# A decayed running sum over a matrix product: seven block products in one of 32 groups, and a list scheduler for slots 34 to 243

## The chip, the cores and the metric

One Trainium2 core runs the whole kernel. The metric is the device time of one launch in microseconds (us), lower is better. Engines: PE (TensorE, matmuls into PSUM), DVE (VectorE), ACT (ScalarE), POOL (GpSimd) and SP, which here only issues the stores.

## What is computed

```python
B, S, D = 16, 2048, 1024          # x: B x S x D, w: D x D, decay: D, all float32
xw = x @ w
out[:, 0, :] = xw[:, 0, :]
for t in range(1, S):
    out[:, t, :] = decay[None, :] * out[:, t - 1, :] + xw[:, t, :]
```

So there is one large product (32768 x 1024 by 1024 x 1024) and, down each column of each batch, a linear recurrence in time. The constants lie between 0.05 and 0.95, one for each column.

## The kernel before

**Tiling.** Time is cut into 64 chunks of 512 steps, and two chunks of one batch make a group: 32 groups. In each group there are eight tiles, one for each n, the block of 128 output columns; a tile is 128 columns by 1024 time steps, since columns lie on partitions and time runs along them. `slots` numbers the tiles: slot s is group s // 8 and n = s % 8. (The last group is worked as two single chunks, slots 248 to 263.) Group 14 is slots 112 to 119; it is the first half of a batch.

**One chunk of x** passes through four steps. `load` (L105) is four POOL DMAs that also turn it into bf16 (xb, three buffers). `turn` (L115) is a transpose on DVE (xw, two buffers). `part` (L123) is two ACT copies that sort it into xt (bf16, 4 x 2 x 512 columns, five buffers). Then 128 matmuls read each pair of chunks. In the written orders these are the letters L, T, X and Y.

**One tile.** PE does 16 matmuls of 128 x 128 by 512 columns (L131), eight blocks k of the inner size for each of the two chunks, into one of three PSUM buffers ps of two banks. Then the recurrence follows in one of two ways:

- A *paired* tile (three of four) solves pairs of steps. ACT copies ps to xs (`copy`, L185, letter p; three buffers) and makes g, the even-numbered steps times decay (`odd`, L170, g). POOL adds g to the odd-numbered steps (`join`, L205, j). DVE scans those 512 values with the squared decay (`scan`, L210, S). ACT scales the result (`even`, L170, h) and POOL adds it to fill the other half (`fill`, L253, c). g and h take turns in four buffers h. A small ACT copy or POOL memset (`zero`, L201 or L199, z) sets the value before the tile.
- An *unpaired* tile (one of four, n % 4 = 3) is one DVE scan of 1024 steps straight from ps (L228).

Either way the last value is kept for the next group of the batch (`save`, L257, k; only in the first half of a batch). DVE transposes the finished line so (four buffers) into ot (`back`, L265, B). After four tiles, SP stores ot (four buffers) in four DMAs (L289). The squared decays lie in a PSUM bank, so that the short scan has one operand there.

**What sets the order.** Every instruction is pinned to the order in which the program issues it, on each engine by itself; buffers and data make engines wait for each other by semaphores. Around slots 0 to 33 and from slot 244 on, the order is written out by hand in `agenda`, a list of letters for each slot. In between `usual` (L522) writes it by one rule: the tile's own copy, scaled half and join, then scan, end and outgoing transpose of the tiles before, then the chunk work that `later` has put at that slot, then one or two loads. `rest` (L536) does what is left over at slot 244.

Of the kernel before, what the change touches and what calls it, by code (L numbers as in the profile page):

```python
# [25 lines left out]
def kernel(  # L26
# [41 lines left out]
    CR = CH // NQ  # L68

# [24 lines left out]
    def ot_tile(nj):  # L94
        return ring(sb, "ot", 4, [128, nj, CR])

# [22 lines left out]
    def part(c, copy, m0, m1, j0=0, j1=NJ):  # L119
        if c not in xt_of:  # L120
            xt_of[c] = ring(sb, "xt", 5, [128, M, 2, TL], BF16)
        src = xw_of[c][:, m0:m1, j0:j1].rearrange("p m j i e -> p m e (j i)")
        pin(copy(out=xt_of[c][:, m0:m1, :, j0 * P:j1 * P], in_=src))  # L123
# [17 lines left out]
    class Tile:  # L141
# [3 lines left out]
        def __init__(self, g, n, ps, outlets):  # L145
# [7 lines left out]
            self.lot = sum(t.paired for t in tiles)  # L153
            self.prev = None if self.t0 == 0 else last[n]
            if self.t0 + self.T < S:
                last[n] = const.tile([128, 1], FP32, name=f"keep{n}", bufs=2)
                self.keep = last[n]
            else:
                self.keep = None

        @property
        def so(self):
            if not hasattr(self, "held"):
                self.held = sb.tile([128, 2 * TL + 2], FP32, name=f"so{self.turn % 4}")
            return self.held

        def decayed(self, src, h=None):
            if h is None:
                h = ring(sb, "h", 4, [128, TL])[:, 0:self.T // 2]
# [12 lines left out]
        def copy(self):  # L182
            self.xs = sb.tile([128, 2 * TL], FP32, name=f"xs{self.lot % 3}")[:, 0:self.T]
            for t, ps in self.parts():
                pin(nc.scalar.copy(out=self.xs[:, t:t + ps.shape[1]], in_=ps))  # L185

        def odd(self):
            self.g = ring(sb, "h", 4, [128, TL])[:, 0:self.T // 2]
            for t, ps in self.parts():
                size = ps.shape[1]  # L190
                self.decayed(ps[:, 0:size:2], self.g[:, t // 2:(t + size) // 2])

# [3 lines left out]

        def zero(self):
            if self.prev is None:
# [4 lines left out]
        def join(self):  # L203
            odds = self.xs[:, 1:self.T:2]
            pin(nc.gpsimd.tensor_tensor(out=odds, in0=self.g, in1=odds, op=ALU.add))  # L205

        def scan(self):
            T, n, so = self.T, self.n, self.so
            if self.paired:
# [3 lines left out]
                    data1=self.xs[:, 1:T:2],  # L213
                    initial=0.0 if self.prev is None else self.prev,
# [7 lines left out]
        def run(self, ps, t, size):  # L222
# [3 lines left out]
            else:  # L226
                before = 0.0 if self.prev is None else self.prev
# [13 lines left out]
        def complete(self):  # L241
# [3 lines left out]
            if self.keep is not None:  # L245
                self.save()

        def even(self):
            self.h = self.decayed(self.so[:, 1:self.T + 1:2])

        def fill(self):
            T = self.T
            pin(nc.gpsimd.tensor_tensor(  # L253
                out=self.so[:, 2:T + 2:2], in0=self.h, in1=self.xs[:, 0:T:2], op=ALU.add))

        def save(self):
            pin(nc.scalar.copy(out=self.keep, in_=self.so[:, self.T + 1:self.T + 2]))  # L257
# [15 lines left out]
    class Outlet:  # L273


        def __init__(self, ns, nj, half=0, queues=(nc.sync,), pieces=1):
# [3 lines left out]
            self.ot = ot_tile(nj)  # L280
# [135 lines left out]
    def turn_and_load(c):  # L416
# [61 lines left out]
        21: "p20 g20 L S18 X8 j20 B17 B19",  # L478
        22: "L h18 p21 c18 B16 k18 g21 B18 Y8 z20 L j21 S20",
        23: "p22 z21 z22 S21 L h20 g22 T9 c20 h21",  # L480
        24: "k21 k20 j22 S23 X9 L c21 Y9 B20 L",
        25: "B23 k23 p24 B21 g24 z24 j24 S22 z25",
        26: "p25 T10 k22 h22 g25 c22 S24 X10 j25",
        27: "B22 p26 S25 g26 z26 Y10 j26",
# [4 lines left out]
        32: "c29 S31 S30 h30 B29 c30 p32 g32 z32 j32 B30 B31 L L",  # L489
        33: "p33 g33 z33 j33 S32 h32 c32 k32 L L",  # L490
# [22 lines left out]
    later = {}  # L513
    begun = {"T": 12, "X": 11, "Y": 11}
    for c in range(5, nch):
        first = c // 2 * K
        ahead = (7, 6, 4) if c % 2 else (11, 10, 8)
        for letter, a in zip("TXY", ahead):
            if c >= begun[letter]:
                later.setdefault(first - a, []).append(f"{letter}{c}")  # L520

    def usual(s):  # L522
        paired = [t.paired for t in tiles]
        do = [f"P{s}"] if paired[s] else []
        if paired[s - 1]:
            do.append(f"S{s - 1}")
        if not paired[s]:
            do.append(f"S{s}")
        do.append(f"C{s - 1}")
        if paired[s - 2]:  # L530
            do.append(f"B{s - 2}")
        if not paired[s - 1]:
            do.append(f"B{s - 1}")
        return do + later.get(s, []) + ["L"] * (2 if len(loads) > NQ else 1)

    def rest(s):  # L536
        do = [f"S{s - 1}"] if tiles[s - 1].paired else []
        do.append(f"C{s - 1}")
        if tiles[s - 2].paired:
            do.append(f"B{s - 2}")  # L540
        return do + [f"B{s - 1}"] + later.get(s, []) + ["L"] * len(loads)

# [3 lines left out]

    perform(agenda[-99].split())
    spares = [spare] + [ring(psp, "spare1", 1, [128, TL])]
    for step, (g, n) in enumerate(slots):
        T = TL * len(g)  # L550
        left = step - len(slots)
        if n % R == 0:
            ns, nj = range(n, n + R), T // P
            outlets = [Outlet(ns, nj)]
# [54 lines left out]
        do = agenda.get(step, agenda.get(left) if left >= -20 else None)  # L609
        if do is None:  # L610
            do = usual(step)
# [34 lines left out]
```

## Time and profile before

| | before |
|---|---|
| median of 3 runs | 904.96 us (904.68 to 905.02) |
| the profiled execution | 905.68 us |
| its span | 903.9 us |
| busy: PE, DVE, ACT, POOL | 896.4, 825.5, 686.3, 656.7 us |
| granted PE clock | 0.999 |
| matmuls | 4217 recorded |
| DMA | 204.77 MB moved, 227 GB/s in the mean |
| a load of x: issue to landing | 7.9 us in the median |
| a store: issue to landing | 10.9 us in the median |

The profile is one execution, recorded instruction by instruction. A line names a group: source line, engine, operation, what is written and read, shape, count, then busy time, mean time of one in ns and the idle time of the engine ahead of it, with the one that ended it. Starts of neighbours on one engine can lie closer than a duration, since the next instruction begins before the last one has quite ended. The span is the profile's own; the device time has some 1.8 us around it.

### The profile page before, as it was taken

The numbers are of one execution on the slowest core, as the hardware profiler recorded it, in microseconds if no ns is written. First come the engines' busy times: TensorE is split into PE (matmuls) and PEld (weight loads), VectorE is DVE, ScalarE is ACT, GpSimd is POOL, SyncE is SP. The second block draws the span as 40 slices with busy tenths as digits, with TensorE's granted clock in tenths as the row PEclk, the third lists the DMA queues.
The fourth block names the chain that finished last, engine by engine and source line by source line (L and its number), as shares of the span: only waits on it lengthen the run. The fifth ranks groups of instructions, "written<-read, shape, count | busy, mean of one in ns | idle before, by whom it ended". The sixth has DMA issues, their size and how long they took to land.

```text
span 903.9 us, 12113 instructions
## 1 busy us (share of the span) xinstructions
PE 896.4 (99%) x4217; PEld 412.7 (46%) x4217; DVE 825.5 (91%) x628; ACT 686.3 (76%) x957; POOL 656.7 (73%) x755
## 2 busy tenths in 40 slices
PE   8999999999999999999999999999999999999997
PEld 5544444444444444444444444444444444444444
DVE  4999998999999999999998999999999999999997
ACT  4899967777877877877778778778777787787742
POOL 7978678777767768677677677777777776776632
PEclk9999999999999999999999999999999999999999
DMA  9999999999999999999999999999999999999868
GB/s 186 190 215 215 226 256 217 215 237 236 254 242 260 243 251 257 248 237 226 224 237 229 224 229 229 230 224 229 231 227 228 233 232 222 226 233 211 176 143 235
DMA packets 402542, 204.77 MB, mean 227 GB/s; under 512 B 8752, under 2 KB 401456, under 8 KB 402480
## 3 DMA queue, kind: packets, MB, share of 16 engines
q1 hardware_dynamic: 265168, 134.76, 61.0%
q0 software_dynamic: 137024, 68.70, 56.6%
q8 instruction: 33, 0.54, 0.2%
q10 hardware_dynamic: 288, 0.52, 0.2%
q14 instruction: 29, 0.24, 0.1%
HBM read 138.42 MB, written 134.22 MB: 302 GB/s over the span
## 4 chain that ended last, share of the span: by engine, by line
PE 97%; DMA 1%; POOL 0%; issue 0%; DVE 0%; DVEq 0%; POOLq 0%
PE ps L131 96%; DMA xb<-in_x_dram 1%; PE spare L131 1%; POOL xb L105 0%; PE spare L395 0%; PE ps L395 0%; DVE h L399 0%; DVE xw L115 0%; DVEq L115 0%; POOLq L630 0%
## 5 line engine op out<-in xcount | busy, mean ns | idle before, releaser
L131 PE MATMUL ps<-xt,wsb 128*128 128x512 bf16 (+1 forms) x4028 | 866.3, 378 | 0.0
L131 PEld LDWEIGHTS <-wsb 128*128 128x128 bf16 x4168 | 407.5, 98 | 478.0 <-ACT wsb L313 0.8
L205 POOL TENSOR_TENSOR xs<-h,xs 128x512 f32<-128x512 f32 (+1 forms) x190 | 242.8, 1278 | 188.1 <-ACT h L170 85.3
L185 ACT COPY xs<-ps 128x1024 f32<-128x1024 f32 (+1 forms) x190 | 188.9, 994 | 152.9 <-PE ps L131 148.1
L265 DVE STREAM_TRANSPOSE ot<-so 128x1024 f32<-128x1024 f32 (+1 forms) x260 | 300.0, 1191 | 2.1 <-POOL so L199 1.1
L253 POOL TENSOR_TENSOR so<-h,xs 128x512 f32<-128x512 f32 (+1 forms) x190 | 241.0, 1270 | 43.7 <-ACT h L170 27.8
L123 ACT COPY xt<-xw 128x2048 bf16<-128x2048 bf16 (+3 forms) x136 | 242.3, 1790 | 8.7 <-DVE xw L115 8.7
L105 POOL DMA_DIRECT2D xb<-in_x_dram x264 | 174.0, 660 | 5.6 <-DMA xb<-in_x_dram 3.2
L170 ACT ACTIVATE h<-so,dec 128x512 f32<-128x512 f32 (+1 forms) x190 | 145.3, 766 | 28.7 <-DVE so L210 25.2
L115 DVE STREAM_TRANSPOSE xw<-xb 128x2048 f32<-128x2048 f32 (+3 forms) x78 | 147.4, 1901 | 8.0 <-DMA xb<-in_x_dram 7.9
L210 DVE TENSOR_TENSOR_SCAN so<-spare,keep,xs 128x512 f32<-128x512 f32 (+1 forms) x97 | 119.9, 1239 | 26.7 <-POOL xs L205 26.4
L210 DVE TENSOR_TENSOR_SCAN so<-spare,xs 128x512 f32<-128x512 f32 x93 | 113.3, 1219 | 27.4 <-POOL xs L205 24.5
L170 ACT ACTIVATE h<-ps,dec 128x512 f32<-128x512 f32 (+1 forms) x190 | 130.0, 684 | 0.0
L228 DVE TENSOR_TENSOR_SCAN so<-dec,ps 128x1024 f32<-128x1024 f32 x34 | 76.8, 2260 | 1.0 <-ACT h L170 1.0
L228 DVE TENSOR_TENSOR_SCAN so<-dec,keep,ps 128x1024 f32<-128x1024 f32 (+1 forms) x35 | 75.9, 2168 | 0.2 <-issue 0.2
L257 ACT COPY keep<-so 128x1 f32<-128x1 f32 x136 | 25.3, 188 | 9.5 <-DVE so L228 9.0
L201 ACT COPY so<-keep 128x1 f32<-128x1 f32 x97 | 18.4, 191 | 2.7 <-DVE ot L265 2.4
L131 PE MATMUL spare<-xt,wsb 128*128 128x512 bf16 (+3 forms) x60 | 12.6, 329 | 0.0
L131 PE MATMUL ps<-xw,wsb 128*128 128x256 bf16 (+3 forms) x68 | 11.2, 301 | 0.4 <-DVE xw L115 0.4
L199 POOL MEMSET so<- 128x1 f32 x93 | 10.7, 117 | 0.6 <-DVE ot L265 0.6
L331 PE MATMUL spare<-idle 128*128 128x512 bf16 x22 | 6.8, 479 | 1.2 <-DVE idle L321 1.2
L306 POOL DMA_DIRECT2D ot<-in_w_dram x12 | 6.6, 552 | 1.7 <-DMA xb<-in_x_dram 0.8
(39 smaller groups left out, 37.9 us busy)
## 6 DMA issues: line engine op xcount, KB each, us to landing
out_dram<-ot SPq DMA_DIRECT2D x248, 512.0 KB, 10.9
xb<-in_x_dram POOLq DMA_DIRECT2D x248, 256.0 KB, 7.9
out_dram<-ot SPq DMA_DIRECT2D x12, 256.0 KB, 4.2
ot<-in_w_dram POOLq DMA_DIRECT2D x12, 128.0 KB, 5.6
xb<-in_x_dram POOLq DMA_DIRECT2D x8, 128.0 KB, 5.4
out_dram<-xb SPq DMA_DIRECT2D x3, 256.0 KB
xb<-in_x_dram POOLq DMA_DIRECT2D x4, 144.0 KB, 7.0
ot<-in_w_dram ACTq DMA_DIRECT2D x2, 256.0 KB, 5.2
```

Of the source, the lines that this page charges most:

```text
L105: pin(nc.gpsimd.dma_start(out=xb_of[c][quad(q), j0:j1], in_=_ap(x, [[D, P], [P * D, j1 - j0], [1, CQ]], (b * S + t0 + j0 * P) * D + q * CQ)))
L115: pin(nc.vector.transpose(out=dst.rearrange("p (m j i) -> p j m i", m=M, i=P)[:, j0:j1, m0:m1], in_=src.rearrange("p (j m c) -> p j m c", ...
L123: pin(copy(out=xt_of[c][:, m0:m1, :, j0 * P:j1 * P], in_=src))
L131: pin(nc.tensor.matmul(out=ps[:, t0:t1] if ps.shape[1] >= t1 else ps, lhsT=lhs, rhs=rhs, start=(k == 0 and t0 == start), stop=(stop and k ...
L170: pin(nc.scalar.activation(out=h, in_=src, func=mybir.ActivationFunctionType.Copy, scale=dec[:, self.n:self.n + 1]))
L185: pin(nc.scalar.copy(out=self.xs[:, t:t + ps.shape[1]], in_=ps))
L205: pin(nc.gpsimd.tensor_tensor(out=odds, in0=self.g, in1=odds, op=ALU.add))
L210: pin(nc.vector.tensor_tensor_scan(out=so[:, 3:T + 2:2], data0=squares[-1][:, n:n + 1].to_broadcast([128, T // 2]), data1=self.xs[:, 1:T:2 ...
L228: pin(nc.vector.tensor_tensor_scan(out=so[:, t + 2:t + 2 + size], data0=dec[:, n:n + 1].to_broadcast([128, size]), data1=ps, initial=befor ...
L253: pin(nc.gpsimd.tensor_tensor(out=self.so[:, 2:T + 2:2], in0=self.h, in1=self.xs[:, 0:T:2], op=ALU.add))
L257: pin(nc.scalar.copy(out=self.keep, in_=self.so[:, self.T + 1:self.T + 2]))
L265: pin(nc.vector.transpose(out=outlet.ot[:, :, c0:c0 + P], in_=self.so[:, 2 + t0:2 + t0 + nj * P].rearrange("p (i t) -> p i t", t=P)))
```

## The change

**Seven products.** In group 14, tiles are worked in pairs (n = 0 and 1, 2 and 3, ...). Inner size, columns and the two chunks each split in two, so that a pair is a product of 2 x 2 blocks, and it is formed by seven block products instead of eight. A block product is four matmuls of 512 columns. It needs sums of x (three in a new buffer sx, one written over half of the group's second xt; each 128 x 2048 bf16; the first, second and fourth on DVE, the third on POOL, each after the one before) and differences of w (five for each pair, 20 in all, each 128 x 512 bf16, on POOL, spread over 80 us that begin 170 us before the group). The products a1, a2, a3 and a4 accumulate in one PSUM bank of a pair, b1 and b2 in the other, c in the bank spare0. Between them ACT copies partial results to the tile's line (A1, A2, B1, A4, "lift") and DVE adds or subtracts (C, A3, B2, "join"), and the next product of that bank waits for this. The tiles then go on as paired ones, without the copy p. All tiles of groups 13, 14 and 15 are paired.

**Order.** In slots 34 to 243 all work is made into jobs with an engine, a cost, a key (how urgent) and what must come before. `in_order` runs these through a list scheduler: an engine that is free takes the most urgent job that is ready. The order that results is issued; on the chip each engine keeps it and waits by semaphores as ever. At its start, ACT, DVE and POOL are taken as busy for 4.0, 4.5 and 5.5 us, and a sum of x on DVE is put at 2.15 us. One tile in five is unpaired where one in four was.

**Buffers.** xs goes; the copy p is written to so and the work is done there, in seven buffers (four so and three xs before). ot goes from four to three, xt from five to four. The transpose of a chunk is split in two halves. The hand-written slots 21 to 33 move X8 to Y9 later and leave X10, Y10 and the last loads to the scheduler.

```diff
+    OTS, XTS, SOS, HS = 3, 4, 7, 4
+    FROM, TO = 34, 244
+    SUMS, SUMT = ('dve', 'dve', 'pool', 'dve'), -24
+    WBY, WLEAD, WSTEP = "pool", 170, 4
+    SHARE = {-1: 0, 0: 0, 1: 0.06, 2: 0.2, 3: 0.2, 9: 0.2}
+    merged = (14,)
...
-        return ring(sb, "ot", 4, [128, nj, CR])
+        return ring(sb, "ot", OTS, [128, nj, CR])
...
-            xt_of[c] = ring(sb, "xt", 5, [128, M, 2, TL], BF16)
+            xt_of[c] = ring(sb, "xt", XTS, [128, M, 2, TL], BF16)
...
-        def copy(self):
-            self.xs = sb.tile([128, 2 * TL], FP32, name=f"xs{self.lot % 3}")[:, 0:self.T]
-            for t, ps in self.parts():
-                pin(nc.scalar.copy(out=self.xs[:, t:t + ps.shape[1]], in_=ps))
-
-        def odd(self):
-            self.g = ring(sb, "h", 4, [128, TL])[:, 0:self.T // 2]
-            for t, ps in self.parts():
-                size = ps.shape[1]
-                self.decayed(ps[:, 0:size:2], self.g[:, t // 2:(t + size) // 2])
-
...
+        def copy(self):
+            for t, ps in self.parts():
+                pin(nc.scalar.copy(out=self.line[:, t:t + ps.shape[1]], in_=ps))
+
+        def odd(self, spot=None):
+            src = self.line if isinstance(self.ps, tuple) or self.ps is None else self.ps
+            self.g = self.decayed(src[:, 0:self.T:2], spot)
...
-        21: "p20 g20 L S18 X8 j20 B17 B19",
-        22: "L h18 p21 c18 B16 k18 g21 B18 Y8 z20 L j21 S20",
+        21: "p20 g20 L S18 j20 B17 B19",
+        22: "L h18 p21 c18 B16 k18 g21 B18 z20 L j21 S20",
         23: "p22 z21 z22 S21 L h20 g22 T9 c20 h21",
-        24: "k21 k20 j22 S23 X9 L c21 Y9 B20 L",
-        25: "B23 k23 p24 B21 g24 z24 j24 S22 z25",
-        26: "p25 T10 k22 h22 g25 c22 S24 X10 j25",
-        27: "B22 p26 S25 g26 z26 Y10 j26",
+        24: "X8 k21 k20 j22 S23 Y8 L c21 B20 L",
+        25: "B23 k23 p24 B21 g24 z24 j24 S22 X9 z25",
+        26: "p25 T10 k22 h22 g25 c22 Y9 S24 j25",
+        27: "B22 p26 S25 g26 z26 j26",
...
+            for e, queue in ready.items():
+                if idle[e] > now:
+                    continue
+                kept = []
+                while queue and queue[0][2].takes and not spots:
+                    kept.append(heapq.heappop(queue))
+                job = heapq.heappop(queue)[2] if queue else None
+                for one in kept:
+                    heapq.heappush(queue, one)
+                if job is None:
+                    continue
+                if job.takes:
+                    job.spot = spots.pop(0)
+                order.append(job)
+                job.start = now
+                end = idle[e] = now + job.cost
+                if job.locks:
+                    idle["pool"] = max(idle["pool"], now) + job.cost / 2
+                heapq.heappush(events, (end, -1 - len(order), None))
+                for other in job.gives:
+                    heapq.heappush(events, (end + GAP, -1 - len(order), (other.spot,)))
...
+    GAP = 0.19
+    BEGUN = {"pe": 0.0, "act": 4.0, "dve": 4.5, "pool": 5.5}
+    LAND = 11.0
+    STORED = 13.0
+    PASS = 0.2158
+    cost = {"p": .91, "g": .6, "z": .12, "j": 1.27, "S": 1.16, "D": 2.2, "h": .68, "c": 1.27,
+            "k": .11, "B": 1.14, "T": 1.14, "X": 1.79, "L": .66, "half": .5, "both": .62,
+            "sum": 2.15, "wpool": 1.15, "wdve": 1.2, "slow": 4.2}
+    each = R * PASS
+
+    differences = ((1, 0, 1, 1), (1, 1, 0, 0), (0, 0, 0, 1), (0, 1, 1, 1), (1, 0, 0, 0))
+
+    def differ(d, j):
+        k1, n1, k2, n2 = differences[d]
+        one, two = (wsb[:, k * R:(k + 1) * R, n + 2 * j].rearrange("p k q i -> p k (q i)")
+                    for k, n in ((k1, n1), (k2, n2)))
+        by = nc.vector if WBY == "dve" else nc.gpsimd
+        pin(by.tensor_tensor(out=wd[:, d, j], in0=one, in1=two, op=ALU.subtract))
...
+        weights = []
+        for i in range(5 * R if merged else 0):
+            weights.append(Job(WBY, cost["w" + WBY], starts[min(merged)] - WLEAD + WSTEP * i,
+                               lambda i=i: differ(i % 5, i // 5)))
+            weights[-1].locks = WBY == "dve"
+            weights[-1].early = max(16.0, weights[-1].key - 4)
...
+        def chunk(c):
+            need = starts[c // 2] - 21 + (c % 2) * 8
+            if c > 11:
+                quads = [q for cc, q in loads if cc == c] if c <= 14 else range(NQ)
+                got = [Job("pool", cost["L"], need - 28 + 2.5 * q, lambda c=c, q=q: load(c, q),
+                           [turned.get(c - 3)]) for q in quads]
+                for q, a in zip(quads, got):
+                    a.early = max(4.0, need - 3 * 4 * each * R + 2) + q * each * R
+                ends = [(a, LAND + (3 if need < 60 else 0)) for a in got]
+                for half in range(2):
+                    turned[c] = Job(
+                        "dve", cost["T"], need + 2 * half,
+                        lambda c=c, h=half: turn(c, 0, NJ, h * M // 2, (h + 1) * M // 2),
+                        ends + [turned.get(c - 1), part_of.get((c - 2, 1)), turned.get(c)])
+                    if len(got) < NQ:
+                        turned[c].early = 2 * LAND
+                    part_of[c, half] = Job(
+                        "act", cost["X"], need + 3 + 3 * half,
+                        lambda c=c, h=half: part(c, nc.scalar.copy, h * M // 2, (h + 1) * M // 2),
+                        [turned[c], part_of.get((c - 1, half))] + used.get(c - XTS, []))
...
+        def solve(tile, ready, key, banks):
+            s = tile.turn
+            prev = place.get((tile.before.turn, "k")) if tile.before is not None else None
+            gone = place.get((s - SOS, "B"))
+            pos = lambda name, e, c, k, do, after, takes=False: place.setdefault(
+                (s, name), Job(e, cost[c], key + k, do, after, takes))
+            if not tile.paired:
+                end = pos("S", "dve", "D", 3, tile.scan, ready + [gone, prev])
+                banks.append(end)
+            else:
+                if tile.ps is not None or not tile.mixed:
+                    p = pos("p", "act", "p", 0, tile.copy, ready + [gone])
+                    banks.append(p)
+                    ready_xs = [p]
+                else:
+                    ready_xs = ready
+                g = pos("g", "act", "g", .5, None, ready, True)
+                g.do = lambda: tile.odd(g.spot)
+                banks.append(g)
+                z = pos("z", "pool" if tile.before is None else "act", "z", 1, tile.zero,
+                        ready_xs + [prev])
+                j = pos("j", "pool", "j", 1.2, tile.join, ready_xs + [g])
+                j.gives = (g,)
+                S = pos("S", "dve", "S", 1.5, tile.scan, [j, prev])
+                h = pos("h", "act", "h", 4.5, None, [S, z], True)
+                h.do = lambda: tile.even(h.spot)
+                end = pos("c", "pool", "c", 5.5, tile.fill, [h])
+                end.gives = (h,)
+            if tile.kept:
+                pos("k", "act", "k", 3.7, tile.save, [place[s, "S"]])
+            back(tile, end, key)
...
+            b = Job("dve", cost["B"], key + 8, tile.back,
+                    [end, place.get((s, "k"))] + stored.get(lump - OTS, []) + ([first] if first else []))
...
+        def product(out, xs, ws, begin):
+            for k in range(R):
+                pin(nc.tensor.matmul(out=out, lhsT=ws(k), rhs=xs[:, k // 2, k % 2],
+                                     start=begin and k == 0, stop=k == R - 1,
+                                     skip_group_check=True))
...
+            def sums(i, engine):
+                if i == 0:
+                    sx[0] = sb.tile([128, 3, 2, 2, TL], BF16, name="sx")
+                a, b = xt_of[c0], xt_of[c1]
+                S1, S2, S0 = (sx[0][:, k] for k in range(3))
+                out, one, two = ((S1, b[:, 0:2], b[:, 2:4]), (S2, a[:, 0:2], S1),
+                                 (S0, a[:, 2:4], S2), (b[:, 0:2], a[:, 0:2], b[:, 0:2]))[i]
+                flat = lambda x: x.rearrange("p m e t -> p (m e t)")
+                pin(engine.tensor_tensor(out=flat(out), in0=flat(one), in1=flat(two), op=ALU.add))
+
+            done = []
+            for i in range(4):
+                by = SUMS[i]
+                done.append(Job(by, cost["sum" if by == "dve" else "slow"], t + SUMT + i,
+                                lambda i=i: sums(i, nc.vector if SUMS[i] == "dve" else nc.gpsimd),
+                                parts + done[-1:] + used.get("sx", [])))
+                done[-1].locks = by == "dve"
...
+            what = {
+                "a1": ("a", lambda: S(0), w_at(0, n0), True, 0),
+                "a2": ("a", lambda: S(1), w_less(1), False, 3),
+                "b1": ("b", lambda: S(2), w_at(1, n1), True, 4),
+                "c": ("c", lambda: xb_()[:, 2:4], w_less(4), True, 5),
+                "a3": ("a", lambda: xa()[:, 0:2], w_less(2), False, 6),
+                "b2": ("b", lambda: xa()[:, 2:4], w_less(0), False, 8),
+                "a4": ("a", lambda: xb_()[:, 0:2], w_less(3), False, 9),
+            }
+
+            def mult(name, after):
+                where, xs, ws, begin, at = what[name]
+
+                def do():
+                    if name == "a1":
+                        held["ps"] = psp.tile([128, 2 * TL], FP32, name=f"ps{bank % 3}")
+                    if name == "c":
+                        held["c"] = psp.tile([128, TL], FP32, name="spare0")
+                    product(spot(where), xs(), ws, begin)
+                return Job("pe", U, t0 + at * U, do, after)
+
+            def spot(where, held=held):
+                return {"a": lambda: held["ps"][:, 0:TL], "b": lambda: held["ps"][:, TL:],
+                        "c": lambda: held["c"]}[where]()
+
+            def half(i, k, two=two):
+                return two[i].line[:, k * TL:(k + 1) * TL]
+
+            def lift(i, k, where, key, after):
+                return Job("act", cost["half"], key, lambda: pin(nc.scalar.copy(
+                    out=half(i, k), in_=spot(where))), after)
+
+            def join(i, k, where, op, key, after, turned=False):
+                def do():
+                    one, other = half(i, k), spot(where)
+                    pin(nc.vector.tensor_tensor(
+                        out=half(i, k), in0=other if turned else one,
+                        in1=one if turned else other, op=op))
+                return Job("dve", cost["both"], key, do, after)
+
+            gone = [place.get((tile.turn - SOS, "B")) for tile in two]
+            at = lambda name: t0 + (what[name][4] + 1) * U - 8
+            a1 = mult("a1", done + weights + (after_ps[bank - 3] if bank >= 3 else []))
+            A1 = lift(0, 1, "a", at("a1"), [a1, gone[0]])
+            a2 = mult("a2", [A1])
+            A2 = lift(0, 0, "a", at("a2"), [a2, gone[0]])
+            b1 = mult("b1", [a1])
+            B1 = lift(1, 0, "b", at("b1"), [b1, gone[1]])
+            c = mult("c", [after_spare[0], part_of[c1, 1]])
+            C = join(0, 1, "c", ALU.add, at("c"), [c, A1])
+            after_spare[0] = C
+            a3 = mult("a3", [A2])
+            A3 = join(1, 0, "a", ALU.subtract, at("a3"), [a3, B1])
+            b2 = mult("b2", [B1])
+            B2 = join(0, 0, "b", ALU.subtract, at("b2"), [b2, A2], True)
+            a4 = mult("a4", [A3])
+            A4 = lift(1, 1, "a", at("a4"), [a4, gone[1]])
+            after_ps[bank] += [B2, A4]
+            used["sx"] = used[c0] = used[c1] = [a1, a2, b1, c, a3, b2, a4]
+            two[0].mixed = two[1].mixed = True
+            solve(two[0], [C, B2], t0 + 10 * U, [])
+            solve(two[1], [A3, A4], t0 + 11 * U, [])
...
+        if FROM <= step < TO:
+            if step == FROM:
+                steady(outlets)
+            continue
```

## The prediction

> **What bounds the kernel now.** First the page: busy shares, and the chain that ended last.
>
> ```profile
> PE 896.4 (99%) x4217; PEld 412.7 (46%) x4217; DVE 825.5 (91%) x628; ACT 686.3 (76%) x957; POOL 656.7 (73%) x755
> ...
> PE 97%; DMA 1%; POOL 0%; issue 0%; DVE 0%; DVEq 0%; POOLq 0%
> ```
>
> TensorE (PE) is the chain. A busy PE may still be one that waits, so next the view of waits, for PE alone, and the chain in order of time:
>
> ```profile
> PE spare L331 <- DVE idle L321: 1.2, 1, 1.2
> PE spare L331 <- ACT gate L348: 0.7, 1, 0.7
> PE ps L131 <- DVE xw L115: 0.4, 1, 0.4
> ```
>
> ```profile
> 43.64 830.69 PE ps L131 x3848
> ```
>
> These are all of PE's waits, 2.3 us, and all fall before 20 us. From 43.64 us on it runs matmul on matmul: 830.69 / 3848 = 0.2159 us each, so 16 x 0.2159 = 3.45 us for a tile (a slot) and 27.6 us for a group of eight. What lengthens PE's list lengthens the kernel, what shortens it gains at most that, and every new wait of PE adds in full.
>
> How near are the others? The stages view, for two stretches of one group each (columns: PE, weight loads, DVE, ACT, POOL busy, then clock, DMA, GB/s):
>
> ```profile
> 383.20:410.80 27.60, 27.60 (x130) 12.52 (x129) 25.61 (x20) 21.39 (x28) 20.47 (x23) 1.00 1.21 233
> 410.80:438.40 27.60, 27.60 (x129) 12.48 (x128) 25.38 (x18) 21.57 (x32) 20.59 (x25) 1.00 1.18 227
> ```
>
> DVE is the next bound: 25.5 of 27.6 us. Steps, not durations, must be added, for neighbours overlap a little; the timeline gives them as distances between starts:
>
> ```profile
> 392.31 1.28 DVE L210 TENSOR_TENSOR_SCAN so<-spare,keep,xs 128x512 f32<-128x512 f32 x1
> 392.69 1.01 ACT L185 COPY xs<-ps 128x1024 f32<-128x1024 f32 x1
> 393.51 2.29 DVE L115 STREAM_TRANSPOSE xw<-xb 128x2048 f32<-128x2048 f32 x1
> 393.59 0.69 ACT L170 ACTIVATE h<-ps,dec 128x512 f32<-128x512 f32 x1
> 394.18 0.19 ACT L201 COPY so<-keep 128x1 f32<-128x1 f32 x1
> ...
> 395.76 1.28 DVE L210 TENSOR_TENSOR_SCAN so<-spare,keep,xs 128x512 f32<-128x512 f32 x1
> ...
> 397.00 1.25 DVE L265 STREAM_TRANSPOSE ot<-so 128x1024 f32<-128x1024 f32 x1
> ```
>
> On DVE: half-length scan 1.22 (1.20 and 1.24), whole chunk transposed 2.25. The same view has an outgoing transpose at 1.17 (two in 2.33 from 389.97) and the long scan of an unpaired tile at 2.24 (400.40 to 402.64). On ACT: copy 0.90, scaled half 0.59; elsewhere in the view h is 0.66, xt 1.80. Check: 6 x 1.22 + 2 x 2.24 + 8 x 1.17 + 2 x 2.25 = 25.7, against 25.4 and 25.6 measured.
>
> The rows nearest to the new operations, from the groups kept apart by shape:
>
> ```profile
> L205 POOL TENSOR_TENSOR xs<-h,xs 128x512 f32<-128x512 f32 x183 | 237.6, 1298 | 177.5 <-ACT h L170 79.9 <-issue 53.8 <-ACT so L201 39.1
> L205 POOL TENSOR_TENSOR xs<-h,xs 128x256 f32<-128x256 f32 x7 | 5.2, 740 | 10.6 <-ACT h L170 5.4 <-ACT so L201 3.2 <-DVE so L228 2.1
> L313 DVE COPY wsb<-ot 128x512 bf16<-128x512 bf16 x7 | 2.1, 352 | 1.5 <-DMA ot<-in_w_dram 1.5
> L399 DVE COPY xb<-ps 128x512 f32<-128x512 f32 x1 | 0.7, 692 | 0.0
> ```
>
> **The products.** Group 14 falls from 8 x 16 = 128 matmuls to 4 pairs x 7 products x 4 = 112, of the same 512 columns, each loading its weights as before (98 ns, beside PE). 16 x 0.2159 = **-3.45 us**, all on the path. The rest can only take from it.
>
> **The gate before group 14.** Its first product waits for four chained sums of x: two on DVE, one on POOL, one on DVE. These wait for the last xt copy of chunk 29, and with four xt buffers (five before) chunks 28 and 29 can't be copied before group 12's last matmul. Call the end of group 13's products 0: the copies start at -27.6. In group 13, all pairs, ACT has 8 x (0.90 + 0.59 + 0.66) = 17.2 us of tiles, 0.7 of small copies and 4 x 1.80 = 7.2 of xt: 25.1 of 27.6. The list scheduler takes an xt copy when nothing more urgent is ready, and at its key (-18, -15, -10, -7) at the latest. Filling the gaps between tiles puts the last one's end at about -15 (slot 103, group 12's last, is unpaired, so ACT begins free); waiting for its key puts it at -5. A DVE sum (2048 bf16): the bf16 copy row, 512 in 0.35, four times less three fixed parts of 0.13, gives 1.0 below (0.13 from 128x448 in 0.355 and 128x576 in 0.418 us); the f32 transpose of 2048 gives 2.3 above. I take 1.1, nearest to the row of the same type. POOL's sum: slope 0.558 / 256 = 2.18 ns, 1.30 + 1536 x 0.00218 = 4.65 above; half, were bf16 read two at a time, 2.3 below; I take 4.65, POOL's only row. Four hand-overs at 0.14 (394.28 ACT end, 394.42 POOL start) make 3 x 1.1 + 4.65 + 0.56 = 8.5. The sums end between -6.5 and +3.5; one product (0.86, the one that needs no sum) covers the first 0.86. Evenly spread: 0.26 x 1.3 = 0.35 us lost on average; with sums of 2.3, 3.6 later, 0.62 x 3.1 = 1.9. Four to one: **+0.7 us**. From both sides: 0 and 6.2.
>
> **Inside group 14.** Products now wait for ACT to lift or DVE to join earlier results. By the order of nine places of 0.86 us, the lifts (a 512-column ACT copy lasts 0.59 among the groups by shape, less 0.09 of overlap: 0.50) have 1.73 - 0.50 - 0.28 = 0.95 us of cover and the join of a3 has 1.73 - 0.69 - 0.28 = 0.76 (0.69: the L399 row). A lift that meets an xt copy just begun (28% of ACT's time, 1.8 long) misses: 0.28 x 0.47 x 0.42 = 0.06, 8 times; a join behind a 1.2 us DVE step: 0.37 x 0.23 = 0.09, 4 times. **+0.8 us**; at worst each: 8 x 0.85 + 4 x 0.46 = 8.6; at best 0, if other products are always put between.
>
> **Load of DVE, ACT, POOL around it.** DVE, group 13: 8 x 1.22 + 8 x 1.17 + 4 x 1.17 (half transposes) + 3 x 1.1 = 27.1; group 14: 23.8 + 12 x 0.69 = 32.1; together 59.2 in 51.8: 7.4 us overdrawn. It hides behind what may be late: with seven so buffers an outgoing transpose may be 16 us late, and chunk 31's last transpose, keyed 11 us before group 15, can be 9.5 late. So nothing; with sums of 2.3 it is 11.0, and 1.5 appears. ACT over both: 25.1, and in group 14 16 lifts of 0.50, 8 x 1.25, 0.8 and 7.2, 26.0: 51.1 of 51.8, nothing. POOL: 20 weight differences of 512, at 1.30 by the L205 row (0.65 if half) = 26 us in the 80 us that they are spread over; free there 80 x (1 - 21.5/27.6) = 17.7 (21.5: 20.5 and 0.4 more pairs of 2.58). It falls 8.3 behind; four h buffers hold about 5 us of its queue, and the three PSUM buffers give 6.9 - 1.5 = 5.4 more. Hidden; without that cover 8.3 appears. POOL in groups 13 and 14: 8 x 2.58 + 5.3 (eight loads at 0.66) = 25.9 twice, and 4.65: 56.5 in 51.8, 4.7 behind, same cover.
>
> **The other groups.** Unpaired tiles go from 1 in 4 to 1 in 5: DVE 6.4 x 1.22 + 1.6 x 2.24 + 12 x 1.17 = 25.4, as before; ACT +0.9; POOL +1.0. No one passes 27.6: 0. Loads are still 8 POOL issues a group, and the plan allows 11 us to land where the issues view says 7.9; stores stay on SP, 10.9 us to land, and three ot buffers give 41. The copies X8 to Y9, moved 2 to 4 slots later, still precede group 4 by six slots.
>
> **Sum.** -3.45 + 0.7 + 0.8 = -1.95. The profiled execution took 905.68 (span 903.9, 1.8 around it) and would take 903.73; the median of the runs is 0.72 below it, so 904.96 - 1.95 = **903.0 us**.
>
> **Rivals.** (B) *The gain is eaten at the gate.* POOL and DVE get in each other's way: each DVE sum waits for one POOL step of 1.30. The gate then comes 3 x 1.30 = 3.9 later and in the mean costs about 2.2 instead of 0.35, DVE's overdraft rises to 11.3 and shows 1.8: -3.45 + 2.2 + 1.8 + 0.8 = +1.4, with the copies in ACT's gaps -1 : 904 to 906.4, no change. For it: sums sit where POOL is nearly full. Against: none of the DVE rows with POOL at work is drawn out (1.22 to 1.28), but those scans take their second operand from PSUM, so the trace can't decide. The Trainium skill, "SBUF — State Buffer", section "Who interferes with whom", says that a DVE instruction with two SBUF inputs contends with a GpSimd one that reads SBUF, and that the later one is blocked until the other is done; this is the rule that speaks against the change, and by it the sum is B's.
>
> (C) *Slower: the written orders hold one another up in the regular groups.* The list scheduler orders four in-order engines by its own costs: a regular group's DVE work is 6.4 x 1.16 + 1.6 x 2.2 + 12 x 1.14 = 24.6 there and 25.4 by rows. In ACT's list an h that waits for a late scan holds back the next tile's PSUM copy, and PE waits once that is over 5.4 us late. If of the 0.75 us per group 0.25 reaches PE, the 25 regular groups lose 6.3: -1.95 + 6.3 = +4.4, 909.3. It decides from (3.45 - 1.5 + 1.8) / 25 = 0.15 us a group. For: ACT's waits for scans reach 3.9 us already. Against: DVE at 92% costs PE nothing today.
>
> (D) *The seven products bring nothing*, since short accumulations run slower than 0.2159 each: 905.0. Against: the matmuls of 512 columns keep that pace over all of the chain.
>
> **How the numbers follow.** Forecast 45%: 901.5 (nothing lost) to 903.15. B 27%, C 25%, D 3%. A measurement of this kernel can tell about 0.2%, 1.8 us, from no change. So faster 0.45, same 0.30 (B and D), slower 0.25. The range goes from 901.5, nothing lost, to 908.0, which takes in the upper costs of gate, lifts and DVE, and the smaller half of C; about 15% lie outside.
>
> **What would show it.** PE's waits should name only the sums' first product (under 2 us, near 400 us) and lifts or joins in group 14 (under 1). POOL's bf16 differences should be near 1.3, DVE's sums 1.1; sums of over 2 with POOL steps beside them are B. PE waits spread over slots 34 to 111 and 120 to 243 are C. The forecast is wrong if PE waits for more than 1.65 us in all, or if the last xt copy of chunk 29 ends later than 8 us before group 14.

## The result and the profile after

The changed kernel takes 918.2 us (median of 4 runs, 914.0 to 921.7) against 904.9: a ratio of 1.0145, 95% interval [1.0102, 1.0189]. It is slower, clear of the noise, and by more than the range on record allowed. The profiled execution took 921.73 us, 16.05 more than the one of before. The page, with the shares of the chain:

```profile
PE 894.7 (97%) x4120; PEld 412.0 (45%) x4201; DVE 814.6 (89%) x695; ACT 716.3 (78%) x1021; POOL 724.5 (79%) x815
...
PE 65%; DMA 7%; DVE 6%; issue 4%; POOL 4%; SPq 3%; ACT 3%; DVEq 0%; POOLq 0%; ACTq 0%
```

PE has lost its monopoly of the chain: 65% where it was 97%, and DMA and SP's queue are in it. PE is still busy 97% of the span, so the busy share alone shows little. The view of waits does (engine and line, what it waited for, us in total, times, longest); first two of PE's, then one of DVE's:

```profile
PE ps L138 <- ACT h L184: 11.5, 5, 5.9
PE ps L753 <- ACT so L829: 1.8, 3, 0.8
```

```profile
DVE ot L276 <- DMA out_dram<-ot: 25.1, 6, 9.9
```

L753 is group 14's products: 1.8 us. The 11.5 us belong to ordinary tiles. And the kernel before had no wait at all like DVE's: six transposes stood, 25.1 us in all, because the ot buffer that they write had not yet been stored. The chain of the longest, in order of time (start, length, what):

```profile
170.12 4.73 SPq L305
...
174.90 4.72 SPq L305
...
179.66 18.36 DMA out_dram<-ot
...
199.31 1.20 DVE ot L276
200.52 1.11 DVE so L221
201.63 1.14 DVE xw L122
...
202.79 1.90 ACT xt L130
...
205.69 0.60 ACT h L184
...
206.33 1.44 PE ps L138 x3
```

Read it from the top. A store is four DMAs that SP issues one after another, and here issuing one takes 4.7 us; the last then needs 18.4 us to land, at 198.0. Only now may DVE write that buffer again; it had stood for 9.9 us. Scan, chunk transpose, xt copy, copy and scaled half follow, and PE, which waited 5.9 us for them, starts again at 206.3. It does not run at full speed at once. Five stages (PE busy with its matmuls second, granted clock third from the end):

```profile
206.40:214.00 7.60, 7.38 (x25) 3.03 (x26) 7.12 (x6) 6.15 (x10) 6.25 (x8) 0.72 1.07 225
...
207.00:210.00 3.00, 2.78 (x7) 1.06 (x7) 2.52 (x3) 3.00 (x3) 1.96 (x3) 0.50 0.94 178
...
435.00:520.00 85.00, 84.33 (x385) 38.27 (x392) 78.42 (x68) 75.49 (x112) 78.36 (x85) 1.00 1.20 222
...
531.00:537.00 6.00, 6.00 (x21) 2.38 (x21) 6.00 (x6) 6.00 (x6) 5.98 (x8) 0.72 0.96 186
...
532.00:534.00 2.00, 2.00 (x6) 0.76 (x5) 2.00 (x2) 2.00 (x2) 2.00 (x3) 0.50 0.97 191
```

After each of the two long PE waits (5.9 us, and 4.35 before 530.9) there is a stretch at a granted clock of 0.50, in which matmuls start 0.43 us apart, about twice the 0.2159. In the mean of the two longer stretches the clock is 0.72, so 0.28 x 7.6 + 0.28 x 6.0 = 3.8 us were lost after the waits were over. The Trainium skill, "TensorE: Matmul & The Clock Gate", Part 1, says that the clock falls to half after an idle window of about 3.4 us and rises after a busy one; the trace agrees for these two waits. It is no safe limit, though: in one run below (`seven28_lent`) a wait of 2.9 us was followed by half clock too.

The account goes from start to start of the matmuls. (The view of waits lists some 0.16 us less for each wait: it counts from the end of the matmul before, drawn 0.38 us after its start, though the next could have started after 0.2159.) Seven waits of ordinary tiles cost 13.5 us, the slow clock 3.8 and waits inside group 14 2.5; the products saved 3.45; the start and the end together came 0.2 earlier. The sum is +16.2, and the device times of the two profiled executions are 16.05 apart.

### The profile page after: what moved, and what is told of

It reads as the page before. It is cut to its first block, busy times and chain, and to the rows that moved or that the text cites. A ratio compares the mean times of both kernels' runs of the same rounds, so it can differ in the third digit from the quotient of the medians.

```text
span 919.9 us, 11960 instructions
## 1 busy us (share of the span) xinstructions
PE 894.7 (97%) x4120; PEld 412.0 (45%) x4201; DVE 814.6 (89%) x695; ACT 716.3 (78%) x1021; POOL 724.5 (79%) x815
## 4 chain that ended last, share of the span: by engine, by line
PE 65%; DMA 7%; DVE 6%; issue 4%; POOL 4%; SPq 3%; ACT 3%; DVEq 0%; POOLq 0%; ACTq 0%
PE ps L138 62%; DMA out_dram<-ot 5%; SPq L305 3%; DVE so L221 2%; PE ps L753 2%; DVE ot L276 2%; DMA xb<-in_x_dram 2%; DVE xw L122 1%; POOL so L264 1%; POOL so L216 1%; ACT h L184 1%; ACT xt L130 1%; POOL xb L112 1%; ACT so L202 1%; PE spare L138 1%
## 5 line engine op out<-in xcount | busy, mean ns | idle before, releaser
L138 PE MATMUL ps<-xt,wsb 128*128 128x512 bf16 (+1 forms) x3821 | 839.8, 379 | 16.7 <-ACT h L184 11.5
L264 POOL TENSOR_TENSOR so<-h,so 128x512 f32<-128x512 f32 (+1 forms) x206 | 263.9, 1284 | 114.0 <-ACT h L184 100.8
L276 DVE STREAM_TRANSPOSE ot<-so 128x1024 f32<-128x1024 f32 (+1 forms) x260 | 305.4, 1192 | 48.6 <-DMA out_dram<-ot 25.1
L216 POOL TENSOR_TENSOR so<-h,so 128x512 f32<-128x512 f32 (+1 forms) x206 | 266.2, 1294 | 66.4 <-ACT h L184 31.7
L202 ACT COPY so<-ps 128x1024 f32<-128x1024 f32 (+1 forms) x198 | 197.5, 998 | 76.5 <-PE ps L138 73.6
L184 ACT ACTIVATE h<-so,dec 128x512 f32<-128x512 f32 (+1 forms) x215 | 165.2, 772 | 46.2 <-DVE so L221 46.1
L122 DVE STREAM_TRANSPOSE xw<-xb 128x1024 f32<-128x1024 f32 (+4 forms) x130 | 152.9, 1191 | 5.6 <-DMA xb<-in_x_dram 5.6
L221 DVE TENSOR_TENSOR_SCAN so<-spare,keep,so 128x512 f32<-128x512 f32 (+1 forms) x106 | 128.5, 1218 | 10.6 <-POOL so L216 10.5
L221 DVE TENSOR_TENSOR_SCAN so<-spare,so 128x512 f32<-128x512 f32 x100 | 119.5, 1199 | 17.5 <-POOL so L216 16.6
L239 DVE TENSOR_TENSOR_SCAN so<-dec,ps 128x1024 f32<-128x1024 f32 x27 | 60.9, 2257 | 3.0 <-PE ps L138 3.0
L239 DVE TENSOR_TENSOR_SCAN so<-dec,keep,ps 128x1024 f32<-128x1024 f32 (+1 forms) x26 | 55.0, 2116 | 1.8 <-PE ps L138 1.6
L620 POOL TENSOR_TENSOR wd<-wsb 128x512 bf16<-128x512 bf16 x20 | 23.1, 1158 | 0.0
L753 PEld LDWEIGHTS <-wd 128*128 128x128 bf16 x80 | 7.8, 97 | 12.0 <-issue 3.2
L753 PE MATMUL ps<-xt,wd 128*128 128x512 bf16 x47 | 11.9, 378 | 0.8 <-ACT so L829 0.7
```

The costliest lines, as they stand in the source:

```text
L122: pin(nc.vector.transpose(out=dst.rearrange("p (m j i) -> p j m i", m=M, i=P)[:, j0:j1, m0:m1], in_=src.rearrange("p (j m c) -> p j m c", ...
L138: pin(nc.tensor.matmul(out=ps[:, t0:t1] if ps.shape[1] >= t1 else ps, lhsT=lhs, rhs=rhs, start=(k == 0 and t0 == start), stop=(stop and k ...
L184: pin(nc.scalar.activation(out=h, in_=src, func=mybir.ActivationFunctionType.Copy, scale=dec[:, self.n:self.n + 1]))
L202: pin(nc.scalar.copy(out=self.line[:, t:t + ps.shape[1]], in_=ps))
L221: pin(nc.vector.tensor_tensor_scan(out=so[:, 3:T + 2:2], data0=squares[-1][:, n:n + 1].to_broadcast([128, T // 2]), data1=so[:, 3:T + 2:2] ...
L239: pin(nc.vector.tensor_tensor_scan(out=so[:, t + 2:t + 2 + size], data0=dec[:, n:n + 1].to_broadcast([128, size]), data1=ps, initial=befor ...
```

## The experiments

Theory A: three ot buffers don't cover a store. Rival B: the work around group 14 overloads DVE and POOL. Rival C, from the prediction: the scheduled orders hold one another up wherever they are used.

**1. The order without the products.** `merged = (14,)` becomes `merged = ()`.

> The scheduled order with its buffers (three ot, four xt, seven so), but no group formed by seven products (the list of such groups is empty). Theory A, DVE waits for a free ot buffer because a store of 4 x 512 KB takes longer to issue and land than three buffers cover: the waits stay, DVE waits over 10 us for stores, and the time is 914 to 926 us (the 14 to 17 us above 905 without the 3.45 saved). Rival B, the work around group 14 (sums, differences, joins) overloads DVE and POOL: the loss goes, 904 to 907 us. Rival C, the written orders hold one another up wherever they are used: 914 to 926 us too, but with PE waits that no store wait precedes.

Measured: 917.45 us, ratio 1.0132 [1.0103, 1.0160], DVE waiting 15.1 us for stores, the longest 9.4 us. The loss is there without any product, sum or difference: B is out as its cause. C is not, by this run alone.

**2. The same with four ot buffers.**

```diff
-    OTS, XTS, SOS, HS = 3, 4, 7, 4
+    OTS, XTS, SOS, HS = 4, 4, 7, 4
-    merged = (14,)
+    merged = ()
```

> As the run with the scheduled order and no seven products, but four ot buffers instead of three (there is room, since the sums and differences are not held). Theory A: no DVE wait for a store, 904 to 907 us. Rival C: 914 to 926 us, unchanged by the buffer. Rival B can't be told from A here.

Measured: 906.54 us, 1.0016 [1.0007, 1.0025]. One buffer is worth 917.45 - 906.54 = 10.9 us. No DVE wait names a store. All of PE's waits, two of them at the start as before:

```profile
PE spare L347 <- DVE idle L337: 1.2, 1, 1.2
PE ps L138 <- DVE so L239: 0.6, 2, 0.3
PE spare L411 <- POOL so L264: 0.4, 1, 0.4
PE ps L138 <- DVE xw L122: 0.2, 1, 0.2
```

From 43 to 855 us the chain is PE alone, with four xt buffers and the scheduled lists. So C is out too. The 1.4 us that this kernel is above the one before come from the end: the 0.6 us of waits lie at 870.9 and 873.1, where the list scheduler hands over to the hand-written slots (from start to start they cost 1.0), and 0.4 us more are lost after that.

**3. The kernel before with three ot buffers**, L95: `ring(sb, "ot", 4, ...)` becomes `ring(sb, "ot", 3, ...)`.

> The kernel before, with three ot buffers instead of four and nothing else changed. Theory A: the same store waits appear in the hand-written order, over 10 us of DVE waiting for stores, 910 to 925 us. Rivals B and C: nothing of theirs is in it, 904 to 907 us.

Measured: 914.24 us, 1.0099 [1.0082, 1.0116]. The hand-written order falls into the same hole. Its chain:

```profile
158.51 4.73 SPq L289
...
163.28 4.79 SPq L289
...
168.11 18.46 DMA out_dram<-ot
...
186.70 0.12 DVE ot L265
...
191.40 8.72 PE ps L131 x29
```

The same 4.7 and 18.4 us, though nothing of the new order is in it: PE waited 5.4 us before 191.4.

**4. Stores made shorter instead of buffers made more.** Of each store only two DMAs are issued; half of the output is not written.

```diff
-                for i, q in enumerate((0, 2, 1, 3)):
+                for i, q in enumerate((0, 2)):
```

The changed kernel so:

> The changed kernel with two of the four DMAs of every store left out, so half of the output is not written and all else is as it was. Theory A (a store takes too long for three ot buffers): no waits for stores, PE loses only what it loses in group 14, about 2.5 us, so 905 - 3.45 + 2.5 + about 1.4 of the plan = 905 to 906.5 us. Rival D (the third buffer makes a wait that does not depend on how long a store takes, for instance an order of transposes that crosses itself): 914 to 922 us, as the changed kernel.

The kernel before with three ot buffers so:

> The kernel before with three ot buffers and two of the four DMAs of every store left out (half of the output is not written). Theory A: 904 to 906 us, against 914 with whole stores. Rival D: 913 to 915 us.

The scheduled order without products so:

> The scheduled order with three ot buffers, no seven products, and two of the four DMAs of every store left out (half of the output is not written). It is the partner of the changed kernel with half of its stores (904.55 us): the difference is what seven products in group 14, with sums, differences and joins, are worth when stores never bind. By the PE waits seen in group 14 (1.8 us named, about 2.5 lost in all) they should be worth 3.45 - 2.5 = 1 to 2 us: 905.5 to 906.5 us. If the load around group 14 (theory B) ate the gain, 904 to 904.6 us.

Measured: 904.55 us (0.9991 [0.9982, 1.0001]), 905.57 (1.0003 [0.9993, 1.0012]) and 906.60 (1.0016 [1.0007, 1.0025]). The first came out below the expected range and the third above it, each by half a microsecond or less. All store waits are gone with three buffers: what counts is how long a store takes. Half the stores also speed the loads (6.6 us to landing in the median, where it was 10.0), and this experiment can't tell the two apart. Experiment 2 against 1, and 3 against the kernel before, do: nothing but the number of buffers changes there. The changed kernel's loss to stores is 918.17 - 904.55 = 13.6 us.

The pair with and without the products differs by 906.60 - 904.55 = 2.05 us, but that is not what the products are worth. In the changed kernel with half of its stores, the 124 matmuls from the first to the last product take 29.31 us (so they do in the changed kernel itself), where 124 x 0.2159 = 26.77: of the 3.45 saved, 2.5 are lost again, and 0.9 is left. The rest of the difference lies elsewhere: the run without products loses 1.0 us at 871 to 873, where its list hands over, and the one with them does not.

**5. The whole change with four ot buffers.** A fourth buffer takes 16 KB more of each partition, and room for it is made elsewhere. First, so goes from seven to six and the sums borrow a turn of the ot ring:

```diff
-    OTS, XTS, SOS, HS = 3, 4, 7, 4
+    OTS, XTS, SOS, HS = 4, 4, 6, 4
...
-                    sx[0] = sb.tile([128, 3, 2, 2, TL], BF16, name="sx")
+                    room = ot_tile(2 * NJ).rearrange("p j c -> p (j c)").bitcast(BF16)
+                    sx[0] = room[:, 0:12 * TL].rearrange("p (k m e t) -> p k m e t", k=3, m=2, e=2)
```

> The changed kernel with four ot buffers; for the room, so has six buffers instead of seven and the sums of x borrow one turn of the ot ring during group 14. Theory A: no or little waiting for stores; the seven products pay, 901.5 to 904.5 us. Rivals B and C: 913 to 922 us as in the changed kernel.

Measured: 914.84 us, 1.0096 [1.0071, 1.0121]: a miss. The early store waits are gone, but while the fourth buffer is lent, one comes back, and lands on the sums:

```profile
394.37 1.25 DVE L276 STREAM_TRANSPOSE ot<-so 128x1024 f32<-128x1024 f32 x1 [6.68 <-DMA out_dram<-ot]
```

```profile
405.90 1.86 PE L753 MATMUL ps<-ot,wd 128*128 128x512 bf16 x4 [3.81 <-ACT so L830]
```

Then the same in group 24 (`merged = (24,)`):

> Seven products in group 24 instead of group 14, with four ot buffers, six so and the sums in a borrowed turn of the ot ring. In the run with group 14 that borrowed turn left three buffers at a time when stores were slow, and one wait of 6.7 us came of it. Theory A: group 24 lies where the changed kernel never waited for a store, so no such wait: 904 to 907 us (906.5 of the plan with four buffers, less 3.45, and 1 to 3 us of waits in group 24). Rival B (the load of sums, differences and joins costs it, wherever the group lies): 911 to 916 us.

Measured: 911.87 us, 1.0062 [1.0045, 1.0079]. A miss again, and the time lies in the range that was expected of rival B, as that of the run before it does. The trace names a store first: the lent turn brought a store wait of 4.8 us at 668.9, just before the sums; in the group that follows PE waits 3.1 us for DVE's joins and 3.0 for ACT's lifts. That the place had been free of store waits in one run of another kernel was no assurance. Against B as the cause in the changed kernel stands experiment 4: with sums, differences, lifts and joins all in it, and no store wait, PE loses 2.5 us inside group 14 and nothing in the other groups.

**6. Four ot buffers, all else kept, the differences of w left out** (the products read w itself, so group 14 does not hold the right result; the tile of the differences goes too, which frees 20 KB):

```diff
-    OTS, XTS, SOS, HS = 3, 4, 7, 4
+    OTS, XTS, SOS, HS = 4, 4, 7, 4
...
-        wd = const.tile([128, 5, R, R, 128], BF16, name="wd")
+        wd = None
...
-        for i in range(5 * R if merged else 0):
+        for i in range(0):
...
-                return lambda k: wd[:, d, j, k]
+                return w_at(differences[d][0], 2 * j + differences[d][1])
```

> Seven products in group 14 with four ot buffers of their own, seven so and sx as in the changed kernel; the room comes from leaving out the 20 differences of w (the products read w itself, so group 14 is not the reference's). Theory A: no wait for a store, 904 to 907 us: 906.5 of the plan with four buffers, less 3.45, and 1 to 3 us of waits in group 14. Rival B in the form that sums and joins are the loss: 911 to 916 us.

Measured: 903.46 us, 0.9980 [0.9971, 0.9989]. It is 906.54 - 903.46 = 3.1 us faster than experiment 2, but that again holds 1.0 us of loss at the hand-over, which this run does not have (at the start it loses 0.4 that the other does not). Inside group 14 the 124 matmuls take 27.76 us, 1.0 over 26.77, so seven products, sums, lifts and joins pay 2.5 us of the 3.45 when no buffer is short; PE's named waits for lifts are 0.2 us. Why 2.5 us are lost there in the changed kernel and 1.0 here was not separated: the differences are gone, but the buffers differ too.

**7. Two tries at the whole change with room from elsewhere.** In the first, loads take two xb buffers from chunk 15 on, the third holds 8 KB of the differences, and so goes to five:

```diff
-    OTS, XTS, SOS, HS = 3, 4, 7, 4
+    OTS, XTS, SOS, HS = 4, 4, 5, 4
...
-            xb_of[c] = ring(sb, "xb", 3, [128, NJ, CQ], BF16)
+            turn_of = c % 3 if c < 15 else (c - 15) % 2
+            xb_of[c] = sb.tile([128, NJ, CQ], BF16, name=f"xb{turn_of}")
...
-                           [turned.get(c - 3)]) for q in quads]
+                           [turned.get(c - 3 if c < 17 else c - 2)]) for q in quads]
```

> The whole change with four ot buffers all the time. The room is found elsewhere: from chunk 15 on, loads take turns in two xb buffers instead of three, the third holds part of the differences of w, and so has five buffers instead of seven. Theory A (only the ot buffer was short): no wait for a store, and the 903.5 us of the run without differences come back with the differences in, 903 to 905 us. Against it stands that fewer xb and so buffers may make waits of their own, then 906 us and more, with PE waits that name loads or outgoing transposes.

Measured: 918.50 us, 1.0154 [1.0138, 1.0170]: a miss. No store wait; most of the loss has moved into group 14, whose 132 matmuls from first to last product take 40.13 us where 28.50 would do:

```profile
PE ps L764 <- ACT so L840: 3.7, 2, 3.5
PE ps L764 <- DVE so L846: 3.0, 2, 1.8
PE ps L764 <- POOL sx L781: 2.1, 1, 2.1
```

The last of the three names the gate of the prediction: sums that come 2.1 us late. So the load around group 14, rival B's, does cost PE where there are fewer buffers to hide it. Three waits of PE before 81 us, 2.8 us in all, point to the five so buffers, since no load of chunk 15 is issued before 140 us; for group 14 it was not separated whether the xb or the so buffers are to blame. In the second, group 28 is formed by seven products, and one ot buffer holds 16 KB of differences from 170 us before it on (`merged = (28,)`, `ot_tile` then turns over the other three):

> Seven products in group 28 instead of group 14; four ot buffers until 170 us before that group, three from then on (the fourth holds differences of w), seven so, three xb. In the changed kernel no DVE wait for a store came after 530 us, with three buffers. Theory A: 903 to 906 us if stores stay fast enough there; each store wait that does come costs PE up to its length, and half clock after it (the changed kernel lost 5.9 and 3.4 us so), so 908 to 913 us with one long one.

Measured: 916.26 us, 1.0128 [1.0107, 1.0149]: a miss. Its store waits are short (0.3 and 1.0 us), but the chain into the group's first long PE wait (2.9 us at 792.4) runs from a store that took 16.7 us to land at 771.9 through DVE's transposes and sums: DVE had no slack there. A second PE wait, 3.2 us at 859.3, has another chain of DVE and ACT work, and its root was not found. No kernel here that computes the whole output beats the one before.

## Why the prediction was wrong, point by point

- **Products, -3.45: right.** The 112 matmuls that nothing holds up start 0.2159 us apart, as forecast. Their net was forecast as -1.95 and is -0.9 in group 14 (experiment 4). That the pair of whole runs differs by 2.05 us, close to the forecast, is luck: more than half of it lies outside group 14.
- **The gate, +0.7: measured as 0.** The last xt copy of chunk 29 ended at 394.24, 15.3 us before a1 (forecast: between 15 and 5), and a1 did not wait for the sums. With half of the stores it ended 16.3 us before. DVE's and POOL's rows show that rival B's rule was at work all the same (start, length):

```profile
394.27 1.23 DVE L770 TENSOR_TENSOR sx<-xt 128x2048 bf16<-128x2048 bf16 x1 [0.98 <-ACT xt L130]
395.00 1.66 POOL L264 TENSOR_TENSOR so<-h,so 128x512 f32<-128x512 f32 x1 [1.25 <-ACT h L184]
395.54 2.20 DVE L770 TENSOR_TENSOR sx<-xt,sx 128x2048 bf16<-128x2048 bf16 x1
396.62 2.28 POOL L216 TENSOR_TENSOR so<-h,so 128x512 f32<-128x512 f32 x1
```

  The first sum takes 1.23 us (forecast 1.1), the second 2.20 while POOL's 1.30 us additions are drawn out to 1.66 and 2.28; the fourth took 1.84. The Trainium skill, "SBUF — State Buffer", section "Who interferes with whom", says that a DVE instruction with two SBUF inputs contends with a GpSimd one that reads SBUF; the trace agrees, with 2.20 us for 1.23. The three DVE sums took 1.6 us longer than three of 1.23, where rival B had 3.9. The early copies covered it: the fourth sum ended at 405.3, 4 us before a1.
- **Inside group 14, +0.8: too small by 1.7.** Three waits for lifts cost 2.25 us from start to start (1.8 in the view of waits), two short ones of 0.15 the rest of the 2.5. The steps themselves were sized well: lifts took 0.59 (forecast 0.59), joins 0.65 to 0.69 (0.69). The chance that a lift comes late, or how late, was put too low; which of them was not found out.
- **Load of the engines, 0: right outside group 14.** With short stores PE loses nothing in the other groups. Whether the load makes the lifts late inside it is open. POOL's differences took 1.16 us each (forecast 1.30), its sum 4.08 (4.65).
- **The step that failed** is the sentence "stores stay on SP, 10.9 us to land, and three ot buffers give 41". Both numbers were wrong, and so the term for store waits, put at nothing, was 13.6 us. 41 us comes out as three times 13.8, the time in which four tiles fill a buffer; but a buffer is taken from the first of its four transposes, not from the store. In the stretch shown the last transpose of one store ended at 164.4, and the next one into that buffer was due when DVE fell idle at 188.3: 24 us. And 10.9 us is the median time from issue to landing of one DMA. Four are issued in turn: the first at 165.4, the fourth at 179.7, 14.3 us later, and this one took 18.4 to land: 198.0, or 33.6 us after the transpose.

  The trace of the kernel before shows how little room there was (transposes as start, length; of the store's DMAs the last two):

```profile
168.97 2.33 DVE L265 STREAM_TRANSPOSE ot<-so 128x1024 f32<-128x1024 f32 x2
...
L289 SPq DMA_DIRECT2D out_dram<-ot x2: 3361/3479/3597, 199.0 to 202.7; - x2
...
DMA to landing us min/median/max: 11.7/11.9/12.1
...
217.43 1.25 DVE L265 STREAM_TRANSPOSE ot<-so 128x1024 f32<-128x1024 f32 x1
```

  The last transpose into one buffer ended at 171.3. Its store stood behind others in SP's queue; its four DMAs were issued from 192.2 to 202.7, and the fourth landed at 214.4, 43.1 us after the transpose. The next transpose into that buffer, four fills on, began at 217.4: 3.0 us to spare. One buffer fewer takes 13.8 us away. The prediction also has "every new wait of PE adds in full"; the two long ones added more, 5.9 and 4.35 us of wait and 3.8 of slow clock.
- **Rival C named the right sign for the wrong reason,** and 909.3 us where 918.2 were measured. The regular groups lost time, but to stores, not to lists that wait for one another: with four buffers the same lists cost PE nothing between 43 and 855 us.
- **The other groups, 0: right for the order, once stores have room.** The scheduled order without products costs 906.54 - 905.16 = 1.4 us, but at its end; in the regular groups it costs nothing.

## What to carry to other kernels

The cover of a ring of buffers is the time from the last write into one to the first write of its next turn, and what must fit under it is the whole release: every issue in its queue and the slowest landing, not a median of one transfer. When a change takes a buffer away, work this out from the busiest stretch of the trace before, even if that trace shows no wait: a wait that isn't there tells nothing of how near it is. And count a stall of PE that lasts several microseconds at more than its length, for the clock. When two runs are subtracted to price one part, look in the traces whether the difference lies in that part.

## What the runs showed of the hardware

- Issuing one store DMA of 512 KB from SP took between 0.3 and 6.1 us in the same kernel (the changed one), and its landing 5.0 to 18.8 us.
- Eight PE waits of 2.9 to 7.4 us, in six of the runs, were each followed by 6 to 12 matmuls that start 0.43 us apart; in the changed kernel the granted clock of such stretches is 0.50. PE waits of up to 1.3 us (`group24_ot4`) were followed by none.
- A DVE addition of 128 x 2048 bf16 with both inputs in SBUF took 1.23 to 2.20 us, and POOL's additions beside it went from 1.30 to 2.28 us.
